# Prompt attention of a hybrid decoder layer: value products of two units in one run, and the merge's small products moved to other PSUM banks

## The chip, the cores and the metric

The kernel runs on one core of a Trainium2 chip. A core has five engines that run side by side and are tied together by semaphores only: TensorE (matrix products; PE in the profile, with PEld for its weight loads), VectorE (DVE), ScalarE (ACT), GpSimd (POOL) and SyncE (SP, which here only issues DMAs). [...] The metric is the device time of one execution in microseconds, lower is better.

## The reference, cut to what matters

The kernel computes one layer of a decoder for a prompt of 2048 tokens and for 8 sequences of 8 new tokens: two mixers in parallel (dilated window attention and a gated linear attention), an output projection, and a feed-forward block with a small convolution. The change touches only the prompt's part of the window attention:

```python
PATTERNS = ((128, 1), (512, 4), (2048, 16))     # window, dilation
def dilated_prompt(q, k, v, window, dil):       # 8 heads of 64
    n = window // dil                           # 128 in each pattern
    qb, kb, vb = to_blocks(q), to_blocks(k), to_blocks(v)
    kk, vv = with_prev(kb), with_prev(vb)       # the block before and the block itself
    s = jnp.einsum('brhcie,brhcje->brhcij', qb, kk) * (E ** -0.5)
    s = jnp.where(mask, s, NEG)
    lse = jax.nn.logsumexp(s, axis=-1)
    p = jnp.exp(s - lse[..., None])
    o = jnp.einsum('brhcij,brhcje->brhcie', p, vv)
    ...
def combine_patterns(results):                  # weights: the softmax denominators
    w = jax.nn.softmax(lses, axis=0)
    return jnp.sum(w[..., None] * outs, axis=0)
```

So each of the three patterns has 16 blocks of 128 queries for each head; a block meets the keys of the block before it and its own (the first block of a strided sequence, and every block of the last pattern, only its own). The outputs of the patterns are merged for each head and position with weights from the softmax denominators.

## The kernel before

The program runs in three stages: the projections and the linear attention, the prompt attention (`attention()`, with `at_merge()` and the class `AtUnit`), and the tail (output projection and feed-forward). The framework's scheduler gives each engine the order of its instructions from the data's dependences, program order as priority, and the buffers that are free: each tile has a tag with so many buffers, and a tile takes one when its first instruction is placed. Over that the kernel lays orders of its own: `line()` in `AtUnit` chains all TensorE instructions of the attention units in program order, and `line()` of the layer does so for GpSimd's gathers and merge work. TensorE's products of the merge are in neither chain; the scheduler puts them between.

The work of `attention()`: four head pairs `pr`, each with three patterns `pat`, each with four groups `g` of four blocks. A group is cut into two units of two blocks in patterns 0 and 1, and is one unit of four blocks in pattern 2. So a head pair has 8 + 8 + 4 = 20 units, and all have 80. A unit has three steps:

- `qk_()`, scores: for each of the two heads a PSUM tile `pas` (tag "as"), filled by products of f32r queries with the high and the low part of the keys (L1860; 8 products of up to 256 columns in patterns 0 and 1, 16 of 128 columns in pattern 2). VectorE adds the mask and takes the row's minimum (L1865: `ass`, `aml`; the queries carry a negative sign), ScalarE takes the exponential with the row's sum (L1869). In patterns 1 and 2 the queries come from a tile `aqg` that GpSimd gathers (`at_gather`, L1130), two for each group, two groups ahead.
- `t()`, transposes: for each head up to four 128x128 transposes of `ass` into a PSUM tile `pat` (L1886, tag "apt", two banks); the tile is copied to SBUF (`apt`) by ScalarE (L63) or VectorE (L65), three to two.
- `pv()`, value products: 64 rows of output for each head, head 0 to partitions 0 to 63 and head 1 to 64 to 127, with 128x64 weights (L1903), 12 or 16 products a unit. The PSUM tile `pao` (tag "ao", two banks) belongs to a group: both units of a group fill it in patterns 0 and 1. After the group's last unit VectorE copies it to `aop` (L65), one SBUF tile for each pattern, in five buffers.

A list `fifo` staggers the steps: when unit n has done its scores, unit n-2 does its transposes and unit n-3 its value products. In TensorE's order the steps come as scores(n), transposes(n-2), values(n-3), scores(n+1), and so on.

When the last unit of a head pair has done its value products, `at_merge()` begins for that pair, a generator that goes on by one step with each group of the next pair. It spreads the row minima and sums of patterns 0 and 2 over the positions with eight small products each (L1139 from `ML[0]`, L1142 from `ML[2]`) into one PSUM tile `pam`, which VectorE multiplies with masks (L1148, L1151) and reduces; a chain of small operations of VectorE and one exponential gives the weights, which TensorE transposes (L1194, into `pab`), VectorE copies and GpSimd's queue writes to memory (`awd`, L1199). They are read back spread over partitions (`awb`, L1187), and GpSimd multiplies the outputs with them and adds (L1229, L1214, L1239), in one order with the gathers of the next pair. For the last pair there is no memory trip: weights are copied out by ScalarE and GpSimd (L1222, L1224), transposed by TensorE into `pab` (L1226), and VectorE multiplies from PSUM (L1227).

The eight PSUM banks before: three for "as", two for "apt", two for "ao", one for "am" (`pam` and the first `pab`; in the last merge `pab` goes round "am", "ao", "ao").

Of the kernel before, what the change touches and what calls it, by code (L numbers as in the profile page):

```python
# [10 lines left out]
F32 = mybir.dt.float32  # L11
# [25 lines left out]
class Layer:  # L37
# [370 lines left out]
    def sweep_a(self, c):  # L408
# [39 lines left out]
        for nn in range(2):  # L448
            wv = [self.wget(), self.wget()]
            for t0, m in self.vblocks(c):  # L450
                ps = self.psum.tile([128, 512], F32, name=self.n("pv"), tag="g1", bufs=3)
                self.vgemm(ps, xs, t0, m, wv)
                vs = self.st.tile([128, 256], F32, name=self.n("vs"), tag="vs", bufs=self.AB["vsb"])
                self.evac(vs[:m], ps[:m, :256], "v")
# [499 lines left out]
        yield  # L954


    AB = dict(mw=1, qg=5, vsb=5, mq='p', klh=1, q=2, v=6, s=6, pt=4, op=5, ps=3, ppt=2, po=2, am=1, skew=(2, 3), man=(), ea=3, ed=5, mp=12, aa=(1, 4, 7, 9, 10), ms='pppp', mv=2, em=1)

    def px(self, name, dt=F32):
        return self.pxpool.tile([128, 2 * H], dt, name=self.n(name), tag="px", bufs=4)  # L960
# [22 lines left out]
    def attention(self):  # L983
        with ExitStack() as ctx:
            self.aq[1] = self.pool(ctx, "at1")
            p = self.ap = self.pool(ctx, "at")
            self.app = self.pool(ctx, "atp", bass.MemoryType.PSUM)
            self.ev = 0
            pend = None
            fifo = []  # L990
            sk = self.AB["skew"]

            def drain(n):
                nonlocal pend
                if len(fifo) > sk[0]:
                    fifo[-1 - sk[0]].t()
                while len(fifo) > n:
                    un = fifo.pop(0)
                    un.t()
                    un.pv()  # L1000
                    if un.last:
                        for _ in pend or ():
                            pass
                        pend = self.at_merge(un.pr, un.ML, un.OP)

            if self.AB['man']:
                eng = mybir.EngineType
                ctx.enter_context(self.tc.manual_schedule(engines={getattr(eng, e) for e in self.AB['man']}))
            self.vq = []
            self.at_loadv(0)  # L1010
            self.at_loadv(1)
            for _ in self.at_load(0, ((1, 2),), to=self.qk0):
                pass
            rest = self.at_load(0, ((2, 4),), to=self.qk0)
            self.qgn = []
            for _ in range(self.AB["qg"]):
                p.tile([128, 4, 128], F32R, name=self.n("aqg"), tag="aqg", bufs=self.AB["qg"])
            for pat in range(3):
                for _ in range(2):
                    p.tile([128, 16, 4], F32, name=self.n("aml"), tag=f"aml{pat}", bufs=2)  # L1020
            for _ in range(2):
                p.tile([128, 3, 4, 128], F32, name=self.n("awb"), tag="awb", bufs=2)
            for _ in range(2):
                p.tile([128, 512], F32, name=self.n("amo"), tag="amo", bufs=2)
            pre = iter(())
            for pr in range(4):
                if pr == 3:
                    self.rctx.close()
                    pre = self.wo_pre()
                qk = self.qk0  # L1030
                nxt = self.at_load(pr + 1) if pr < 3 else iter(())
                ML, OP = [], []
                for pat in range(3):
                    base = 16 * (3 * pr + pat)
                    ml = p.tile([128, 16, 4], F32, name=self.n("aml"), tag=f"aml{pat}", bufs=2)
                    op = p.tile([128, 4, 512], F32, name=self.n("aop"), tag="aop", bufs=self.AB["op"])
                    ML.append(ml)
                    OP.append(op)
                    for g in range(4):
                        if base // 4 + g + 2 < 48:  # L1040
                            self.at_loadv(base // 4 + g + 2)
                        for _ in rest:
                            pass
                        po = [None]
                        nu = 1 if pat == 2 else 2
                        for u in range(nu):
                            fifo.append(AtUnit(self, pr, pat, g, u, nu, qk, base, ML, OP, po))
                            fifo[-1].qk_()
                            drain(sk[1])
                            if pat:  # L1050
                                next(pre, None)
                        if pend is not None:
                            next(pend, None)
                        if 5 <= 4 * pat + g < 11:
                            self.qk0 = next(nxt, self.qk0)
            for _ in pre:
                pass
            drain(0)
            for _ in pend:
                pass  # L1060
# [73 lines left out]
    def at_merge(self, pr, ML, OP):  # L1134
        nc, p, pp, AB = self.nc, self.ap, self.app, self.AB
        sel, sm = self.asel, self.asm
        pm = pp.tile([128, 512], F32, name=self.n("pam"), tag="am", bufs=AB["am"])
        for r in range(4):
            nc.tensor.matmul(pm[:, 64 * r:64 * r + 64], sel[r], ML[0].rearrange("p b x -> p (b x)"),  # L1139
                             start=True, stop=True)  # L1140
# [20 lines left out]
        em, line = (nc.gpsimd, lambda x: x) if pr == 3 else (nc.vector, self.line)  # L1161
# [28 lines left out]
            return W  # L1190

        if not last:
            pt = pp.tile([128, 512], F32, name=self.n("pab"), tag="am", bufs=AB["am"])
            nc.tensor.transpose(pt[:96, :128], awf, self.ident)  # L1194
            wt = p.tile([128, 512], F32, name=self.n("awt"), tag="amo", bufs=2)[:96, :128]
            self.evac(wt, pt[:96, :128], "v")
            wd = self.a["awd"][pr]
            yield
            line(nc.gpsimd.dma_start(wd, wt))  # L1199
            yield  # L1200
            nxt = weights(0)
            for _ in range(AB["mw"]):
                yield
        tags = ("am", "ao", "ao")
        j = 0
        for cb in range(4):
            sl = slice(128 * cb, 128 * cb + 128)
            if last:
                W = weights(cb)
            else:  # L1210
                W, nxt = nxt, weights(cb + 1) if cb < 3 else None
            for i in range(3):
                if i == 2 and not last:
                    line(nc.gpsimd.tensor_tensor(OP[1][:, :, sl], OP[1][:, :, sl], OP[0][:, :, sl], op=ALU.add))  # L1214
                    yield
                if last:
                    tg = tags[j % 3]
                    pb = pp.tile([128, 4, 128], F32, name=self.n("pab"), tag=tg, bufs=AB[dict(am="am", ao="po")[tg]])
                    ab = W[:, i].rearrange("p r (h e) -> p r h e", h=2)
                    src = cap(aw, 24 * cb + 4 * i, [[1, 4], [12, 2], [0, 64]])  # L1220
                    if j in AB['aa']:
                        nc.scalar.copy(ab, src)  # L1222
                    else:
                        nc.gpsimd.tensor_scalar(ab, src, 1.0, 0.0, op0=ALU.mult, op1=ALU.add)  # L1224
                    for r in range(4):
                        nc.tensor.transpose(pb[:, r, :], W[:, i, r, :], self.ident)  # L1226
                    nc.vector.tensor_tensor(OP[i][:, :, sl], OP[i][:, :, sl], pb, op=ALU.mult)  # L1227
                else:
                    line(nc.gpsimd.tensor_tensor(OP[i][:, :, sl], OP[i][:, :, sl], W[:, i], op=ALU.mult))  # L1229
                j += 1  # L1230
            if last:
                mo = self.aq[1].tile([128, 512], F32, name=self.n("amo"), tag="ass", bufs=AB["s"])
            else:
                mo = p.tile([128, 512], F32, name=self.n("amo"), tag="amo", bufs=2)
            e, le = (nc.vector, lambda x: x) if last else (nc.gpsimd, line)
            if last:
                e.tensor_tensor(OP[1][:, :, sl], OP[0][:, :, sl], OP[1][:, :, sl], op=ALU.add)
            e, le = (nc.vector, lambda x: x) if last and cb >= AB["mv"] else (nc.gpsimd, line)
            le(e.tensor_tensor(mo.rearrange("p (m r) -> p r m", r=4),  # L1239
                               OP[1][:, :, sl], OP[2][:, :, sl], op=ALU.add))  # L1240
            line(nc.gpsimd.dma_start(self.a["mixa"][:, pr, 512 * cb:512 * cb + 512], mo))
            if last and cb < 2:
                if cb == 0:
                    self.xnext[3] = self.hl()
                o, m = ((0, 512), (512, 2 * H - 512))[cb]
                self.split(*(t[:, o:o + m] for t in self.xnext[3]), mo[:, :m], "v")
            if cb < 3:
                yield
# [807 lines left out]
```

## Time and profile before

| | |
|---|---|
| median of three runs | 2746.82 us (2745.77 to 2751.03) |
| the profiled execution | 2747.31 us; span 2745.3 us, granted clock 0.989 |
| busy over the span | PE 2655.9 us (97%), DVE 1791.5 (65%), ACT 1270.2 (46%), POOL 587.2 (21%) |
| prompt attention | about 770 to 1063 us of the span |

A row of the order of time gives start, length, engine, line, operation, `out<-in`, and in brackets the idle time before it and what ended that. Lengths of TensorE's products overlap, since they are pipelined; what a product costs is read from start to start. In the view of windows each engine has its busy time in a stretch and the number of instructions, then come the clock granted to TensorE (1.00 is full), the share of the DMA engines and GB/s. In the view of waits the columns are total us, times, and the longest.

### The profile page before, as it was taken

To read this page: it belongs to the slowest core of one execution; us is meant where nothing else is said; L and a number is where in the kernel's file an instruction comes from. 1 tells how busy PE (TensorE), PEld (TensorE's weight loads), DVE (VectorE), ACT (ScalarE), POOL (GpSimd) and SP (SyncE) were. 2 spreads that over 40 slices of the span, in tenths; PEclk is the share of its full clock that TensorE was granted. 3 is DMA by queue.
4 is the path that set the end of the run, shared out by engine and by line. 5 is a ranking of instruction groups with operands and counts; after the bars stand their busy time and mean duration, and the time that the engine had idled before them with its cause. 6 is when DMAs were issued, how large, how long until landed. Compare 5 with 4: busy or idle time off the path is not lost. (4 is left out here: it accounts for less than half of the span.)

```text
span 2745.3 us, 58213 instructions
## 1 busy us (share of the span) xinstructions
PE 2655.9 (97%) x22203; PEld 2520.9 (92%) x22203; DVE 1791.5 (65%) x4338; ACT 1270.2 (46%) x2961; POOL 587.2 (21%) x643
## 2 busy tenths in 40 slices
PE   8999999999999998998999998999999999999997
PEld 6899899888788887998999998999999999999997
DVE  7545544444357776468899889865676665766666
ACT  6535433333368784445555455433344332443332
POOL 4435243433345674012000020000110000200001
PEclk9999999999999999999999999999999999999998
DMA  8755436799776663376677588986698766976654
GB/s 316 254 182 190 165 116 218 264 334 370 267 260 193 191 168 108 127 249 258 249 274 288 196 323 299 341 303 207 239 341 289 279 227 211 327 249 216 215 192 148
DMA packets 287015, 661.67 MB, mean 241 GB/s; under 512 B 32960, under 2 KB 82752, under 8 KB 284688
## 3 DMA queue, kind: packets, MB, share of 16 engines
q1 hardware_dynamic: 256528, 579.53, 61.1%
q0 software_dynamic: 13216, 46.56, 5.1%
q10 hardware_dynamic: 16992, 31.86, 3.1%
q8 instruction: 175, 2.87, 0.4%
q14 instruction: 104, 0.85, 0.1%
HBM read 511.45 MB, written 146.37 MB: 240 GB/s over the span
## 5 line engine op out<-in xcount | busy, mean ns | idle before, releaser
L70 ACT ACTIVATE ws<-wr 128x512 fp32r<-128x512 f32 (+1 forms) x482 | 292.8, 616 | 426.2 <-PE pfe L1628 138.6
L92 PE MATMUL pfd<-hh,ws 128*128 128x264 f32 x2816 | 474.6, 285 | 6.8 <-ACT ws L70 5.6
L92 PEld LDWEIGHTS pfd<-hh,ws 128*128 128x128 f32 x2816 | 400.0, 189 | 9.2 <-ACT ws L70 7.4
L73 DVE TENSOR_TENSOR ws<-wr,ws 128x512 fp32r<-128x512 f32 (+1 forms) x482 | 319.4, 668 | 119.5 <-ACT ws L70 115.7
L92 PE MATMUL pfd<-hl,ws 128*128 128x264 f32 x1408 | 301.5, 285 | 1.8 <-DVE hl L73 1.8
L1628 PE MATMUL pfe<-xh,ws 128*128 128x264 f32 x1496 | 290.3, 286 | 12.1 <-DVE u L1615 7.6
L1628 PE MATMUL pfa<-xh,ws 128*128 128x264 f32 x1496 | 289.8, 285 | 4.5 <-ACT ws L70 1.9
L1628 PE MATMUL pfd<-xh,ws 128*128 128x264 f32 x1408 | 289.3, 285 | 2.1 <-ACT ws L70 1.0
L1628 PEld LDWEIGHTS pfe<-xh,ws 128*128 128x128 f32 x1496 | 236.5, 189 | 13.8 <-DVE u L1615 8.4
L1628 PEld LDWEIGHTS pfa<-xh,ws 128*128 128x128 f32 x1496 | 234.9, 188 | 6.0 <-ACT p L1617 2.4
L399 PE MATMUL pv<-wh,xh 128*128 128x256 f32 (+1 forms) x816 | 236.1, 289 | 1.8 <-DVE th L696 1.8
L1628 PEld LDWEIGHTS pfd<-xh,ws 128*128 128x128 f32 x1408 | 231.3, 189 | 3.1 <-ACT ws L70 1.2
L399 PE MATMUL pv<-wh,xl 128*128 128x256 f32 (+1 forms) x816 | 232.2, 285 | 0.0
L399 PE MATMUL pv<-wl,xh 128*128 128x256 f32 (+1 forms) x816 | 232.2, 285 | 0.0
L92 PEld LDWEIGHTS pfd<-hl,ws 128*128 128x128 f32 x1408 | 225.1, 189 | 2.1 <-DVE hl L73 2.0
L1577 POOL DMA_DIRECT2D xl<-d_xst x52 | 28.1, 541 | 830.8 <-PE pfe L1628 495.4
L1869 ACT ACTIVATE ass<-ass,aml 128x256 f32<-128x256 f32 (+1 forms) x384 | 173.5, 454 | 63.7 <-DVE aml L1865 37.9
L1628 PE MATMUL pfd<-xl,ws 128*128 128x264 f32 x704 | 200.6, 285 | 0.7 <-DMA xl<-d_xst 0.7
L92 PE MATMUL pq<-xh,wh 128*128 128x512 f32 (+2 forms) x480 | 170.9, 364 | 10.7 <-ACT xh L234 7.9
L1628 PE MATMUL pfe<-xl,ws 128*128 128x264 f32 x616 | 175.7, 285 | 0.0
L1628 PE MATMUL pfa<-xl,ws 128*128 128x264 f32 x616 | 174.8, 284 | 0.0
L92 PE MATMUL pq<-xl,wh 128*128 128x512 f32 (+2 forms) x480 | 174.0, 364 | 0.0
(335 smaller groups left out, 6531.6 us busy)
## 6 DMA issues: line engine op xcount, KB each, us to landing
ws<-d_wst SPq DMA_DIRECT2D x248, 512.0 KB, 5.2
wr<-in_wu SPq DMA_DIRECT2D x114, 512.0 KB, 5.0
d_wst<-ws SPq DMA_DIRECT2D x88, 512.0 KB, 4.1
wr<-in_wd SPq DMA_DIRECT2D x160, 256.0 KB, 3.8
wr<-in_wt SPq DMA_DIRECT2D x60, 512.0 KB, 7.0
wh<-d_wbs SPq DMA_DIRECT2D x35, 512.0 KB, 5.6
wl<-d_wbs SPq DMA_DIRECT2D x35, 512.0 KB, 5.8
skp<-in_ckt SPq DMA_DIRECT2D x16, 1024.0 KB, 8.1
```

What stands on the lines that cost most here:

```text
L70: h = nc.scalar.activation(hi, src, AF.Copy)
L73: return h, (nc.gpsimd if lo_eng == "p" else nc.vector).tensor_tensor(lo, src, hi.bitcast(F32), op=ALU.subtract)
L92: mm = nc.tensor.matmul(o, ww[:, k, :], xx[:, s0:s0 + n], start=(k == order[0] and i == 0), stop=(k == order[-1] and i == 2))
L399: mm = nc.tensor.matmul(ps[:m, :256], x[:, t0:t0 + m], w[:, k % 4, :], start=(k == 0 and i == 0), stop=(k == KT - 1 and i == 2))
L1577: self.nc.gpsimd.dma_start(t.bitcast(F32), xo[i, z])
L1628: self.lastmm = nc.tensor.matmul(bank[:, :H], w[:, ww, k, :], xx, start=new and k == 0 and j == 0, stop=k == 3 and j == 2, skip_group_chec ...
L1869: ex = nc.scalar.activation(ssb[:, sc:sc + nk], ssb[:, sc:sc + nk], AF.Exp, bias=self.ml[:, idx, h:h + 1], scale=-1.0, accum_out=self.ml[: ...
```

## The change

Units get a running number `i`. The value products are held back while the newest unit's number is odd; with an even one, the two oldest units do their value products one after the other, and the transposes of unit n-2 come behind them instead of ahead. TensorE's order is then, for even n, scores(n), values(n-4), values(n-3), transposes(n-2), and for odd n, scores(n), transposes(n-2). The tag "as" has four banks for three. The tag "am" is gone: `pam` and the first `pab` take banks of "ao"; in the last merge `pab` goes round "as", "ao", "as".

```diff
-    AB = dict(..., op=5, ps=3, ppt=2, po=2, am=1, skew=(2, 3), ...)
+    AB = dict(..., op=5, ps=4, ppt=2, po=2, skew=(2, 3), ...)
...
+            ui = 0
 
             def drain(n):
                 nonlocal pend
-                if len(fifo) > sk[0]:
-                    fifo[-1 - sk[0]].t()
-                while len(fifo) > n:
+                new = fifo[-1 - sk[0]] if len(fifo) > sk[0] else None
+                while len(fifo) > n and not (n and fifo[-1].i % 2):
                     un = fifo.pop(0)
                     un.t()
                     un.pv()
...
+                if new:
+                    new.t()
...
                             fifo.append(AtUnit(self, pr, pat, g, u, nu, qk, base, ML, OP, po))
+                            fifo[-1].i = ui
+                            ui += 1
                             fifo[-1].qk_()
                             drain(sk[1])
...
     def at_merge(self, pr, ML, OP):
-        pm = pp.tile([128, 512], F32, name=self.n("pam"), tag="am", bufs=AB["am"])
+        pm = pp.tile([128, 512], F32, name=self.n("pam"), tag="ao", bufs=AB["po"])
...
-            pt = pp.tile([128, 512], F32, name=self.n("pab"), tag="am", bufs=AB["am"])
+            pt = pp.tile([128, 512], F32, name=self.n("pab"), tag="ao", bufs=AB["po"])
...
-        tags = ("am", "ao", "ao")
+        tags = ("as", "ao", "as")
...
-                    pb = pp.tile([128, 4, 128], F32, name=self.n("pab"), tag=tg, bufs=AB[dict(am="am", ao="po")[tg]])
+                    pb = pp.tile([128, 4, 128], F32, name=self.n("pab"), tag=tg, bufs=AB[dict(ao="po").get(tg, "ps")])
```

More of the change, by code (lines that the diff above doesn't have):

```diff
@@ L954, in gla_sample @@
         yield
-    AB = dict(mw=1, qg=5, vsb=5, mq='p', klh=1, q=2, v=6, s=6, pt=4, op=5, ps=3, ppt=2, po=2, am=1, skew=(2, 3), man=(), ea=3, ed=5, mp=12, aa=(1, 4, 7, 9, 10), ms='pppp', mv=2, em=1)
+    AB = dict(mw=1, qg=5, vsb=5, mq='p', klh=1, q=2, v=6, s=6, pt=4, op=5, ps=4, ppt=2, po=2, skew=(2, 3), man=(), ea=3, ed=5, mp=12, aa=(1, 4, 7, 9, 10), ms='pppp', mv=2, em=1)
     def px(self, name, dt=F32):
```

## The prediction

> **What bounds the kernel now.** I read the page first, then the stretches of prompt attention in the view of windows, then who waited for whom between 770 and 1050 us, and last the order of time on TensorE and GpSimd.
>
> ```profile
> span 2745.3 us, 58213 instructions
> ```
>
> The profiled execution took 2747.31 us, 0.49 above the median of 2746.82; its span is 2745.3. The change touches only prompt attention, 770 to 1063 us. Windows (columns: PE, PEld, DVE, ACT, POOL busy, granted clock):
>
> ```profile
> 783.30:796.50 13.20, 13.20 (x138) 11.84 (x137) 9.51 (x39) 10.76 (x39) 0.18 (x1) 1.00 0.85 292
> 815.40:831.20 15.80, 15.80 (x167) 14.28 (x166) 11.04 (x72) 15.29 (x70) 6.42 (x6) 1.00 0.55 176
> 831.20:855.40 24.20, 24.19 (x245) 21.33 (x243) 22.92 (x95) 19.92 (x74) 1.79 (x3) 1.00 0.75 230
> 880.30:900.80 20.50, 18.05 (x157) 16.44 (x155) 10.81 (x70) 16.17 (x74) 19.64 (x20) 0.83 0.59 159
> 900.80:925.10 24.30, 24.17 (x247) 21.31 (x245) 23.19 (x97) 18.68 (x68) 8.63 (x10) 1.00 0.80 271
> 1041.10:1063.30 22.20, 14.60 (x120) 11.97 (x119) 17.39 (x30) 7.04 (x14) 16.32 (x27) 0.92 0.24 84
> ```
>
> TensorE is full in most of them, but it is the only full engine in the first alone. In pattern 2 of the first head pair ScalarE is busy 15.29 of 15.80 us; in pattern 0 of a later pair, where the small work of the merge runs beside it, VectorE is busy 22.92 of 24.20 and 23.19 of 24.30; in pattern 2 of the second pair TensorE waits and its clock falls to 0.83. What it waits for:
>
> ```profile
> 893.98 0.48 PE L1860 MATMUL pas<-akh,aqg 128*128 128x128 f32 x1 [2.45 <-POOL aqg L1130]
> 853.61 0.53 POOL L1199 DMA_DIRECT2D d_awd<-awt  x1 [27.70 <-PE pao L1903]
> 892.88 2.04 POOL L1130 CAST aqg<-aqs 128x512 fp32r<-128x512 f32 x2
> 923.22 0.54 POOL L1199 DMA_DIRECT2D d_awd<-awt  x1 [15.21 <-DVE awt L65]
> 964.52 2.02 POOL L1130 CAST aqg<-aqs 128x512 fp32r<-128x512 f32 x2
> ```
>
> GpSimd carries the merge's products and the query gathers in one order. From the write of the weights (853.61) to the pair's last gather (892.88 + 2.04 = 894.92) is 41.3 us; the next round is 923.22 to 966.54, 43.3 us. TensorE arrives early at the last gather and waits. So from the second pair on the time is a loop: GpSimd's 41 to 43 us, then what lies between the last gather and the next write (894.92 to 923.22, 28.3 us), most of it VectorE's.
>
> **What the change saves.** Units have running numbers n (20 per head pair, 80 in all). Before, TensorE runs scores(n), transposes(n-2), value products(n-3). After, for even n: scores(n), values(n-4), values(n-3), transposes(n-2); for odd n: scores(n), transposes(n-2). Nothing is removed; there are 40 runs of value products for 80. What a run costs to enter and leave, from the waits and the order of time:
>
> ```profile
> PEld pao L1903 <- issue: 14.5, 73, 2.0
> PEld pas L1860 <- issue: 9.4, 55, 0.2
> PEld pas L1860 <- DVE aml L1865: 0.5, 3, 0.2
> 842.19 1.04 PE L1886 MATMUL pat<-c_ident,ass 128*128 128x128 f32 x8
> 843.15 0.88 PE L1903 MATMUL pao<-apt,av 128*64 128x128 f32 x12
> 843.96 0.38 PE L1860 MATMUL pas<-akh,aqs 128*128 128x256 f32 x1
> 844.18 0.28 PE L1860 MATMUL pas<-akl,aqs 128*128 128x256 f32 x1
> 845.00 1.26 PE L1886 MATMUL pat<-c_ident,ass 128*128 128x128 f32 x8
> 851.32 0.60 PE L1886 MATMUL pat<-c_ident,ass 128*128 128x128 f32 x4
> 851.75 0.27 PE L1194 MATMUL pab<-c_ident,aaw 128*96 128x128 f32 x1
> 851.86 0.60 PE L1886 MATMUL pat<-c_ident,ass 128*128 128x128 f32 x4
> 852.39 1.09 PE L1903 MATMUL pao<-apt,av 128*64 128x128 f32 x16
> 853.41 0.39 PE L1860 MATMUL pas<-akh,aqs 128*128 128x256 f32 x1
> 773.34 0.82 PE L1886 MATMUL pat<-c_ident,ass 128*128 128x128 f32 x6
> 773.92 0.37 PE L1860 MATMUL pas<-akh,aqs 128*128 128x256 f32 x1
> ```
>
> Start to start: four transposes before another 128-column product take 0.43 us (851.32 to 851.75), four before a value product 0.53 (851.86 to 852.39): entering costs 0.10. Sixteen value products take 1.02 (852.39 to 853.41), twelve 0.81 (843.15 to 843.96), so one is 0.053 to 0.055 and a run carries some 0.15 besides. The first score product after them takes 0.22 (843.96 to 844.18) where the other seven take 0.82, 0.117 each (844.18 to 845.00): leaving costs 0.10. Together 0.35 us a run; the two waits of the weight load on "issue", 14.5 / 73 and 9.4 / 55, about 0.2 and 0.17 us, are its trace. Transposes to scores, of which the new order has two in each pair of units, show no such cost: six transposes took 0.58 (773.34 to 773.92), less than 6 x 0.1075. The new neighbours (scores to values, values to transposes) aren't in the trace. Bounds: 0.20 (the two edges alone) and 0.35; I take 0.35, since the 0.15 belongs to a run, whatever its length. [...]
>
> Gross: 40 x 0.35 = 14.0 us. What of it reaches the end:
> - First pair, patterns 0 and 1 (TensorE alone full): six pairs of units, n = 6 to 16, 6 x 0.35 = **-2.1**.
> - Pattern 2: at most 15.80 - 15.29 = 0.5 us in four units, with ScalarE's queue in order; taken as 0.
> - Between a write of the weights and the last gather: 0. GpSimd covers it; the 2.45 us wait grows by what TensorE saves.
> - Between the last gather and the second half of the merge's sums: one run of values fewer in each of three rounds, 3 x 0.35 = **-1.05**.
> - Beside the merge's small work VectorE leaves 24.20 - 22.92 = 1.3 and 1.1 us a round: 0 to 3 x 1.2 = 3.6; taken as 0, because the chain's operations stand in VectorE's queue between the units'.
>
> **What the change adds.** The transposes' two banks: transposes(n-2) of an odd n now come one scores run (8 x 0.117 = 0.94 us) after the previous ones, where a run of values and one of scores lay between (2.0 us).
>
> ```profile
> 790.42 1.03 PE L1886 MATMUL pat<-c_ident,ass 128*128 128x128 f32 x8
> 791.42 0.56 ACT L63 COPY apt<-pat 128x512 f32<-128x512 f32 x1
> 792.39 0.57 ACT L63 COPY apt<-pat 128x512 f32<-128x512 f32 x1
> ```
>
> Here the second bank's copy ends at 792.96. In the new order the next transposes would need that bank at 790.42 + 8 x 0.1075 + 0.94 + 0.43 = 792.65: a wait of 0.31, and the copies queue behind exponentials. Bounds 0 and 0.3 for each pair of units; 0.2 in nine pairs that count, **+1.8**. The fourth score bank has to cover scores that now follow each other across one run of transposes; scores wait 0.5 us in all for VectorE now (3 times, in the waits above), with one scores run free of every other work between two; with four banks for it: 0.
>
> The merge's sums now take a bank from the two of the value products:
>
> ```profile
> L1139 PE MATMUL pam<-aml,atab x32: 218/275/275, 796.5 to 1002.6; 128*128 128x64 f32 x32
> L1142 PE MATMUL pam<-aml,atab x32: 219/275/323, 835.3 to 1041.9; 128*128 128x64 f32 x32
> 899.31 1.53 PE L1903 MATMUL pao<-apt,av 128*64 128x128 f32 x16
> 901.03 1.28 POOL L1214 TENSOR_TENSOR aop<-aop,aop 128x512 f32<-128x512 f32 x1
> 902.65 2.39 DVE L65 COPY aop<-pao 128x512 f32<-128x512 f32 x2
> L65 DVE COPY aop<-pao 128x512 f32<-128x512 f32 x47 | 38.6, 824 | 11.5 <-PE pao L1903 11.3
> ```
>
> The first half of these sums (L1139) is placed when pattern 0's maxima are there, 39 us ahead of the second (L1142), in a bank that nothing else used. If that stays so, one bank is left to the values through patterns 1 and 2. In pattern 1 both units of a run share a bank; in pattern 2 each has its own, so in the run (n = 16 and 17 of each pair) the second waits for the copy of the first. Cheapest 0 (the sums placed late, or the wait inside ScalarE's backlog); dearest as at 899.31: those values ended before 900.84, their copy began at 902.65, after GpSimd's last read of an output buffer (901.03 + 1.28 = 902.31), and a copy takes 0.82 us on the mean: 902.65 + 0.82 - 900.84 = 2.6 us. I take 0.5 four times, nearer the cheap end, as TensorE has slack in pattern 2: **+2.0**. The transposed weights (L1194) need a bank for one product and a 0.28 us copy: 0.
>
> Ends. The scores of the fifth unit wait for keys:
>
> ```profile
> 780.85 0.38 PE L1860 MATMUL pas<-akl,aqs 128*128 128x256 f32 x1 [0.87 <-DMA akl<-d_kl]
> 1062.19 1.32 PE L1226 MATMUL pab<-c_ident,awb 128*128 128x128 f32 x8 [1.58 <-DVE aop L1227]
> ```
>
> The values that stood ahead of them (12 x 0.055 = 0.66) no longer cover that: **+0.5**. In the last merge the products rotate through six banks for three, and the wait of 1.58 us for VectorE can go; but VectorE is busy 17.39 of 22.20 us there and feeds what follows. Bounds 0 and -1.6; **-0.5**. Queues of DMA and GpSimd keep their order.
>
> Sum: -2.1 - 1.05 + 1.8 + 2.0 + 0.5 - 0.5 = **+0.65** on 2747.31, 2747.96; less 0.49 for the median, 2747.5 us.
>
> **Rivals.** Two executions of this kernel differ by up to 5.3 us, so 0.2% (5.5 us) is the line for "no change".
> - *Faster: the saving isn't swallowed.* VectorE's chain also gives up its 1.2 us a round and the last merge its 1.6, and neither copies nor banks make TensorE wait: 3.15 + 3.6 + 1.6 = 8.4 us, 2738.5. For it: 0.35 us is in every run. Against it: ScalarE, VectorE and GpSimd at 95% and more in turn.
> - *Slower: the held bank.* The second value product of pattern 2 waits 2.6 us in three rounds and 1.0 in the first pair (the copy and its start), ahead of the second half of the sums, so that the loop grows: 8.8 in place of 2.0, +7.45 in all, 2754.3. It decides from (5.5 + 1.35) / 4 = 1.7 us in each of the four. For it: 39 us between the two halves. Against it: the scheduler may find no free bank and place the sums late.
> - *The change doesn't do what it says:* the cost hangs on the first products of any new kind of run. Then nothing is saved and the costs stay, +3.8: 2750.6, still within 0.2%.
>
> **How the numbers follow.** No change, with the third rival in it: 0.57. Faster 0.26 (a further 5 us, where 40 runs save nearly all of 14, have 0.05 of that). Slower 0.17. The range leaves out about a tenth at each end: 2739 to 2754; the likeliest case alone is 2743 to 2751.
>
> **What would show it.** Right: values in runs of 28 or 32; "issue" waits of the weight load before them about half of 73; the wait at the last gather longer than 2.45 us; 41 to 43 us from write to last gather unchanged. Wrong: L1139 right beside L1142 in time (then the held bank is no cost); waits of transposes for copies well over 0.2 us a pair; the stretch from last gather to write shorter than 28 us by more than 1 us. I'd be wrong altogether if the scheduler set VectorE's merge chain in another place.

## The result, and the profile after

The changed kernel took 2765.0 us (median of 4 runs, 2762.88 to 2767.45), the kernel before 2746.3 beside it (2741.34 to 2751.03): a ratio of 1.0065, 95% interval 1.005 to 1.008. It is 18.7 us slower, where 2747.5 was forecast with a range that ended at 2754. The profiled execution took 2767.45 us.

```profile
span 2765.4 us, 58199 instructions
```

Of the 20.1 us by which the spans of the two profiled executions differ, 19.0 lie in the attention stage. Scores(n) is the one mark that both orders share, so the table gives the time from the first scores of one unit to those of another (worked out from the order of time on TensorE; the last column ends at the first product behind the attention). Units 0 to 19 are the first head pair; in a later one eight units are pattern 0 (the previous pair's merge is worked out beside them), eight are pattern 1, four are pattern 2.

| us | first pair | pattern 0, pairs 2, 3, 4 | pattern 1, pairs 2, 3, 4 | pattern 2, pairs 2, 3 | last four units and last merge | all |
|---|---|---|---|---|---|---|
| before | 61.2 | 25.2, 25.3, 25.4 | 23.9, 23.8, 24.3 | 20.4, 22.5 | 41.2 | 293.2 |
| after | 60.3 | 32.9, 34.9, 33.2 | 21.7, 21.7, 26.4 | 18.0, 20.2 | 42.8 | 312.2 |

Pattern 0 of the three later pairs takes 25.1 us more, the rest 6 us less. Some 2.5 us of both only changed place: the first eight of the sums' products, 0.84 us a round, stood in pattern 1 before (860.55 us) and stand in pattern 0 of the next pair now (840.99). The same in the view of windows (PE, PEld, DVE, ACT, POOL busy, then the granted clock), pattern 0 of the second and third pair; in the kernel before, TensorE was busy 25.24 of 25.25 us in the first of the two:

```profile
829.60:862.50 32.90, 26.96 (x270) 25.05 (x269) 24.86 (x101) 21.18 (x81) 4.88 (x6) 0.90 0.67 198
902.21:937.13 34.92, 28.09 (x270) 25.71 (x269) 24.63 (x101) 20.70 (x78) 15.39 (x16) 0.90 0.78 251
```

TensorE is no longer full there, and its clock has fallen (0.90 in both rows, 1.00 in the kernel before). What it waits for, in the view of waits (engine, tile, line, what ended the wait: us in all, times, longest); line numbers behind the change are 4 higher than before:

```profile
PE pab L1198 <- DVE aaw L1184: 15.9, 3, 5.3
PEld pat L1890 <- issue: 7.5, 40, 0.3
PEld pao L1907 <- issue: 3.3, 7, 2.0
```

The transposed weights, costed at nothing, stand for 15.9 us. Of the short waits of the weight load ahead of value products, 73 before, 7 are left; 40 ahead of transposes are new. The order of time on TensorE around the first of the three waits for the weights:

```profile
840.99 1.00 PE L1143 MATMUL pam<-aml,atab 128*128 128x64 f32 x8
841.83 1.06 PE L1146 MATMUL pam<-aml,atab 128*128 128x64 f32 x8
842.72 1.04 PE L1890 MATMUL pat<-c_ident,ass 128*128 128x128 f32 x8
844.42 0.28 PE L1864 MATMUL pas<-akl,aqs 128*128 128x256 f32 x1
850.04 0.42 PE L1198 MATMUL pab<-c_ident,aaw 128*96 128x128 f32 x1 [5.34 <-DVE aaw L1184]
850.39 3.26 PE L1907 MATMUL pao<-apt,av 128*64 128x128 f32 x28
853.58 1.66 PE L1890 MATMUL pat<-c_ident,ass 128*128 128x128 f32 x8
857.93 1.97 PE L1907 MATMUL pao<-apt,av 128*64 128x128 f32 x32
```

and VectorE's chain from the sums to the weights in that time:

```profile
842.98 0.42 DVE L1152 TENSOR_TENSOR atm<-pam,atab 128x256 f32<-128x256 f32 x1 [0.31 <-issue]
846.90 0.18 DVE L1168 TENSOR_TENSOR amm<-amm,aw 128x32 f32<-128x32 f32 x1
848.26 0.21 DVE L1178 TENSOR_TENSOR adn<-aaw,aw 128x32 f32<-128x32 f32 x1 [0.73 <-ACT aaw L1175]
849.46 0.44 DVE L1184 TENSOR_TENSOR aaw<-aaw,amm 128x32 f32<-128x32 f32 x3
```

Sums and transposed weights now take their banks from the value products' pool of two, and here TensorE's order keeps the order in which the banks were asked for: the sums (all 16 products together), a run of transposes and one of scores, the transposed weights, and only then the next value products. VectorE needs 6.9 us for the weights, from 842.98 to 849.90 (849.46 + 0.44). TensorE stands for 5.34 us, and the value products and transposes behind it, which need nothing of the weights, stand with it. No other product ran in the 5.34 us, and no weight load either: the one of the transposed weights, at 850.01, has 5.52 us of idle time before it. Behind the wait the clock is down, 0.52 from 850 to 855 us: 28 value products take 3.26 us at 850.39, and at full clock 32 take 1.97 at 857.93.

```profile
850.00:855.00 5.00, 4.96 (x38) 4.43 (x38) 1.25 (x3) 0.00 (x0) 3.14 (x4) 0.52 0.59 214
855.00:860.00 5.00, 5.00 (x61) 4.69 (x60) 3.41 (x18) 4.38 (x14) 1.75 (x3) 1.00 0.79 172
```

### The profile page after: what moved, and what is told of

The parts are those of the page before. It is cut to its first block, busy times and chain, and to the rows that moved or that the text cites. A ratio compares the mean times of both kernels' runs of the same rounds, so it can differ in the third digit from the quotient of the medians.

```text
span 2765.4 us, 58199 instructions
## 1 busy us (share of the span) xinstructions
PE 2653.6 (96%) x22203; PEld 2530.7 (92%) x22203; DVE 1795.4 (65%) x4338; ACT 1269.8 (46%) x2961; POOL 585.5 (21%) x643
## 5 line engine op out<-in xcount | busy, mean ns | idle before, releaser
L70 ACT ACTIVATE ws<-wr 128x512 fp32r<-128x512 f32 (+1 forms) x482 | 293.2, 616 | 433.2 <-PE pfe L1632 137.9
L1660 DVE TENSOR_TENSOR acc<-acc,pfd 128x264 f32<-128x264 f32 x304 | 116.4, 422 | 90.9 <-PE pfd L92 90.5
```

What stands on the lines that cost most here:

```text
L70: h = nc.scalar.activation(hi, src, AF.Copy)
L1660: nc.vector.tensor_tensor(acc[m][:, s0:s0 + n], acc[m][:, s0:s0 + n], pz, op=ALU.add)
```

## Experiments

Each ran beside the kernel before on the same chip; ratios are to those runs (medians of before from 2743.0 to 2746.1), with 95% intervals. Two theories were set against each other. A: the transposed weights' product, through the bank that it shares, is what costs. B: it is the order of the units, or the sums.

**order_only**: the new order alone, with the banks as they were.

```
     AB: ps=3, po=2, am=1                      # as before
     pam, pab: tag="am"; tags = ("am", "ao", "ao")
...
+    new = fifo[-1 - sk[0]] if len(fifo) > sk[0] else None
+    while len(fifo) > n and not (n and fifo[-1].i % 2):
...
+    if new:
+        new.t()
```

> Kernel before with the new order of value products alone: scores keep three banks, the merge's sums and transposed weights keep their own bank. Theory A (the loss of 19 us is TensorE standing 5.3 us, three times, at the transposed weights that a value bank has put ahead of value products, the slow clock behind that, and the last merge's sums coming 23 us later): the loss is gone, no wait of TensorE for the weights; with the saving of the first head pair, 2740 to 2748 us, if three score banks cost little; each scores run that follows a transposes run alone then waits for VectorE's reads. Theory B (transposes and scores too close together for the copies and reads): still slower than before, 2755 us or more.

Measured: 2742.03 us, ratio 0.9995 (0.9982 to 1.0007), no change. The third transposed weights stand between transposes and wait for nothing:

```profile
990.59 0.27 PE L1198 MATMUL pab<-c_ident,aaw 128*96 128x128 f32 x1
990.70 1.04 PE L1890 MATMUL pat<-c_ident,ass 128*128 128x128 f32 x8
```

**banks_only**: the changed banks with the old order.

> Kernel after with the old order of value products: four score banks, sums and transposed weights in the banks of the value products. Theory A: slower than before: the transposed weights again stand ahead of value products of the next pair, one run of values later than in the kernel after, so TensorE waits some 2 to 4 us three times, and the last merge's sums come behind most of the last value products: +6 to +18 us, 2752 to 2764. Theory B: as before, 2744 to 2749.

Measured: 2770.43 us, 1.0096 (1.0081 to 1.0111). The banks alone cost 27 us. The transposed weights wait 4.67, 4.68 and 4.68 us, more than was put down for theory A. So the loss comes with the banks, and the new order takes some of it back.

**wtrans_late**: the changed kernel, the transposed weights one step later in the merge's program.

```
+            yield
             pt = pp.tile(... name=self.n("pab"), tag="ao", bufs=AB["po"])
...
             wd = self.a["awd"][pr]
-            yield
```

> Kernel after, with the transpose of the weights one step of the merge (two units) later in program order; the write of the weights keeps its place. Theory A: TensorE meets the transpose two units later, the wait of 5.3 us falls to 0 to 2 us three times and the clock no longer falls behind it; the last merge is untouched: 2748 to 2757. Theory B: 2763 to 2767, as after.

Measured: 2753.37 us, 1.0029 (1.0014 to 1.0044). The waits are 2.24, 2.25 and 2.24 us, a little more than theory A gave. The clock stays up behind the first and the third (32 value products take 1.97 us) and falls to half for 3.4 us behind the second (3.00 us). By the ratios about half of the loss is gone (1.0065 to 1.0029).

**last_sums_as**: the changed kernel, the last pair's sums in a score bank.

> Kernel after, with the sums of the last merge alone in a bank of the scores, which are done by then. Theory A: the sums are ready some 6 us earlier, the last merge starts that much earlier: 2757 to 2762. Rival (the end of attention hangs on the last value products and VectorE's copies of them, not on the sums): 2764 to 2766.

Measured: 2760.99 us, 1.0063 (1.0039 to 1.0087). The last sums come 8 us earlier in the stage, VectorE begins on them 4 us earlier, and the stage ends no earlier (313.3 us against 312.2): the last merge doesn't hang on them. The median lies in the theory's range, but the kernel before also ran 3.3 us lower beside this one than beside the change; the ratios, 1.0063 and 1.0065, show no gain.

**weights_own**, **sums_own**, **shared_three**: three score banks, and the freed bank for the transposed weights alone, for the sums alone, or for nothing.

```
weights_own:  ps=3, am=1;  pam: tag="ao";  pab: tag="am"
sums_own:     ps=3, am=1;  pam: tag="am";  pab: tag="ao"
shared_three: ps=3;        pam: tag="ao";  pab: tag="ao"
```

> The changed kernel with three score banks again and the freed bank for the transposed weights alone; the sums stay in a value bank. In the order of issue the one product of the transposed weights then stands between two runs of transposes, behind two more units, and not ahead of a run of values. Theory A (the loss of 18.7 us is this product, which stands in TensorE's order 5.3 us before its operand is ready, three times, and the clock that falls behind it): the three waits are under 0.5 us, the clock stays at 1.00 there, and the time falls to 2744 to 2752. Rival B (the sums in a value bank are what costs, since they come late and all together): the waits go but the time stays above 2756. The last merge keeps its bank order, so if its loss is separate (from the last write of the weights to the end of attention 81.1 us in the changed kernel, 68.4 before), 2750 to 2756, with 74 us or more in that stretch.

> The mirror image: three score banks, the freed bank for the merge's sums alone, the transposed weights stay in a value bank. The sums go back to two halves, some 40 us apart. Theory A: the product of the transposed weights still waits three times for VectorE's weights, 3 to 5.5 us each, and the time stays at 2754 to 2766. Rival B: the time is within 4 us of before (2743), whatever that product waits.

> The changed kernel with three score banks; the fourth is left unused, sums and transposed weights stay in the value banks. It prices the fourth score bank by itself. Theory A (the bank hides little, since scores follow each other across one run of transposes): within 5 us of the changed kernel, 2760 to 2770, with waits of scores for VectorE of 1 to 1.5 us once or twice a head pair. Rival: the fourth bank is what lets TensorE run on, and without it the scores wait in each pair of units, 0.3 us in 40 of them: 2774 and more.

| kernel | sums | transposed weights | us | ratio | pattern 0, pairs 2, 3, 4 |
|---|---|---|---|---|---|
| order_only | own | own | 2742.03 | 0.9995 (0.9982 to 1.0007) | 25.2, 27.0, 26.5 |
| weights_own | shared | own | 2749.58 | 1.0011 (1.0001 to 1.0022) | 25.8, 26.6, 26.5 |
| sums_own | own | shared | 2755.24 | 1.0032 (1.0021 to 1.0044) | 27.7, 34.2, 33.3 |
| shared_three | shared | shared | 2763.45 | 1.0061 (1.0043 to 1.0079) | 32.8, 34.9, 33.3 |

By the ratios the transposed weights' shared bank costs 0.50% (1.0061 less 1.0011) where the sums share too and 0.37% where they don't, 10 to 14 us; the sums' shared bank costs 0.16% and 0.29%, 4 to 8 us. A difference of two ratios is uncertain by about 0.2% here, so the weights' cost is clear of noise and the sums' only just. The two together are the loss, and the fourth score bank is worth nothing: with it 1.0065, without it 1.0061. In weights_own the product is at 851.76 us, between transposes and a whole pair of units behind the sums, with the weights ready 1.7 us before. From the last write of the weights to the end of attention weights_own takes 70.1 us (81.1 in the changed kernel, 68.4 before), so most of the loss in that stretch came from the same product and was not separate. In sums_own the product waits again:

```profile
PE pab L1198 <- DVE aaw L1184: 12.7, 3, 5.0
```

**one_value_bank**: four score banks, one value bank, the merge's bank kept.

```
AB: ps=4, po=1, am=1;  pam, pab: tag="am"
```

> The bank for the fourth score bank taken from the values in place of the merge: four score banks, one value bank, sums and transposed weights in one bank of their own, last merge in five banks. It prices a held value bank, the slower rival of the prediction: in pattern 2 the second unit of each run of values waits for the copy of the first. Rival of the prediction (2.6 us in each such run of a later pair): two runs a head pair, 2 x 2.6 x 3 and 2 x 1.0 in the first = 17.6 us more than with two value banks, 2757 to 2765. If the wait is nearer the 0.5 us that was put in the sum, 8 x 0.5 = 4: 2744 to 2750. In patterns 0 and 1 a run starts 5.7 us after the last one and a copy takes 0.82, so no wait is expected there.

Measured: 2761.51 us, 1.005 (1.0033 to 1.0067), where the prediction's slower rival gave it 2757 to 2765:

```profile
PE pao L1907 <- DVE aop L65: 13.9, 5, 3.9
```

A value run that finds its only bank held by a copy waits some 3 to 4 us: 3.06 and 3.91 us in the third pair's first units (values of pattern 2 of the pair before), 6.8 in all at the same place in the fourth. The second pair has one of 2.93 us there, at 844.13, which the view puts down to another operation of VectorE, though the copy of that bank ended at 844.07. The price of that rival (2.6 us) was near. It did not occur in the change, because the sums were not placed early.

**before_light**, **order_light**: where the saved runs go. Both orders, with the old banks and without the additions of one output buffer to another.

```
-    line(nc.gpsimd.tensor_tensor(OP[1][:, :, sl], OP[1][:, :, sl], OP[0][:, :, sl], op=ALU.add))
```

> The kernel before without the sum of two output buffers in the merges of the first three head pairs: the four additions of aop to aop on GpSimd (1.28 us each) are left out, so the first pattern's share is missing from those pairs. It shortens GpSimd's chain from the write of the weights to the last gather (41.4 us in the last pair) by up to 5.1 us in each of three rounds. Theory A (in the kernel before this chain ends about together with TensorE's own work, TensorE waits 2.0 us at the last gather): the chain shortens, the waits at the last gather go, and the time falls by 3 x 2 and a little more, 5 to 10 us: 2734 to 2740. Rival: the gathers are not what holds TensorE, and nothing changes (within 3 us).

> The new order with the tags' old banks (three score banks, sums and transposed weights in one of their own), and the same additions left out. With them the new order gained nothing (2742.0 against 2743.0). Theory A (what the 40 saved runs bring is swallowed by GpSimd's chain of 41 us in each of three rounds): here more of it reaches the end, and the new order is 4 to 10 us faster than the kernel before with the same omission. Rival (what is saved on the edges of the runs goes elsewhere: to the waits of scores for the third bank, to copies of the transposes, to VectorE's chain): the two orders again agree within 3 us.

Measured: 2727.31 us, 0.9933 (0.9916 to 0.9951), and 2729.86 us, 0.9943 (0.9928 to 0.9958). Taking 5.2 us a round (4 x 1.30) off GpSimd's chain saves 18.8 and 16.2 us: it does set the time of the kernel before. That is more than the 5 to 10 expected and than the 15.6 us taken off in three rounds: with the waits at the gathers the stretches of fallen clock behind them go too (in before the clock is at half for 6.83 us from 893.41 and from 965.09; in before_light it stays up in pattern 2 of both pairs, 1.00 from 850 to 892 us and from 914 to 957). But the new order gains nothing here either. TensorE does its work in less time in it (busy 262.5 us of the stage for 267.0), and waits instead:

```profile
766.64:1041.58 274.94, 266.98 (x2685) 0.99 0.67 195
766.40:1045.55 279.15, 262.48 (x2686) 0.97 0.65 192
947.56 0.33 PE L1863 MATMUL pas<-akh,aqg 128*128 128x128 f32 x1 [2.54 <-POOL aqg L1134]
```

(the first row is the stage of before_light in the view of windows, TensorE alone; the other two are of order_light). The lighter chain still holds the new order at one gather.

**before_light2**, **order_light2**: also without the product of pattern 1 with its weights.

```
-                else:
+                elif i != 1:
                     line(nc.gpsimd.tensor_tensor(OP[i][:, :, sl], OP[i][:, :, sl], W[:, i], op=ALU.mult))
```

> The kernel before with two parts of the merge left out in the first three head pairs: the sum of two output buffers, as in the lighter kernel above, and the product of the second pattern with its weights (4 more operations of 1.28 us on GpSimd a pair). Theory A (GpSimd's chain swallowed the saving; in the lighter kernel TensorE is already busy 270.6 us of its attention stage of 274.9, so it is the bound there): nothing more is gained, 2723 to 2729. Rival: GpSimd still held it, and it gains up to 15 us more.

> The new order with the old banks and the same two parts left out. Theory A: the wait of 2.54 us at a gather and the fallen clock behind it go, TensorE's saving of 7 us in busy time and more reaches the end: 2716 to 2723, 4 to 10 us less than the old order with the same omission. Rival (the new order has a cost of its own: copies of the transposes, the third score bank, the last pair): within 3 us of the old order.

Measured: 2728.21 us, 0.9935 (0.9922 to 0.9948), and 2724.16 us, 0.9921 (0.9908 to 0.9933). The old order gains nothing more: TensorE, busy 267.0 us of its stage as in before_light, is its bound. The new order is 4 us ahead, at the low end of the difference expected; its time lies just above the range of 2716 to 2723, and the two intervals overlap, so the gain isn't clear of noise. The stage of the profiled executions shows where it would come from:

| us | first pair | pattern 0 | pattern 1 | pattern 2 | last four and merge | all |
|---|---|---|---|---|---|---|
| before_light2 | 61.7 | 25.2, 25.3, 25.3 | 23.9, 23.8, 24.3 | 15.0, 15.0 | 36.7 | 276.1 |
| order_light2 | 59.6 | 25.2, 25.5, 25.5 | 22.5, 22.5, 26.3 | 14.3, 14.4 | 37.2 | 273.1 |

In pattern 1, where TensorE alone is full, the eight units take 22.5 us for 23.85: 0.34 us for each of four saved runs (0.18 to 0.40; most often a pair of units takes 5.25 us for 5.64). In pattern 0 nothing is saved; VectorE is busy 23.7 of 25.2 us there, so it probably sets that time, which no run tried.

**order_old_last**, **old_last_six**: the new order with old banks, the old order in the last pair; and the same with the last merge in score and value banks.

```
+    if new and fifo[-1].i >= 60:
+        new.t()
-    while len(fifo) > n and not (n and fifo[-1].i % 2):
+    while len(fifo) > n and not (n and fifo[-1].i % 2 and fifo[-1].i < 60):
old_last_six also:
-    tags = ("am", "ao", "ao")
+    tags = ("as", "ao", "as")
```

> The new order with the old banks in the first three head pairs, the old order (transposes, then the value products of one unit) in the last pair. In the profiles the new order reached the first scores of the last pair after 196.6 us, the old one after 202.4, and the last pair to the end of attention then took 95.3 and 90.9. If that loss belongs to the order in the last pair, where other work stands beside it on ScalarE and VectorE: 4 us less than the new order throughout, 2736 to 2740. Rival (the last pair's time is set by GpSimd's chain from the third write of the weights, 41 us in both): no more than 1.5 us off, 2741 to 2744.

> The same as the one before, and the last merge's products rotate through the score banks and the value banks (five here) in place of the merge's own and the value banks (three), as the change has it. The prediction put this step of the change at 0.5 us saved, bounds 0 and 1.6. Expected 0 to 1.6 us less than without it; a loss above 1 us would say that the scores' banks come free later than the merge's own.

Measured: 2742.58 us, 0.9988 (0.9977 to 0.9999), and 2744.79 us, 0.9997 (0.9987 to 1.0007). The last pair is not given back by its own order (from unit 60 on 96.4 us, 95.3 with the new order throughout, 90.9 before), so the rival holds. The last merge's banks show no gain; a loss above 1 us can't be told from none.

**before_vadd**, **order_vadd**: the whole computation, the additions on VectorE.

```
-    line(nc.gpsimd.tensor_tensor(OP[1][:, :, sl], ...
+    nc.vector.tensor_tensor(OP[1][:, :, sl], ...
```

> The kernel before, whole, with the additions of two output buffers in the merges of the first three pairs moved from GpSimd to VectorE. GpSimd's chain becomes 5 us a round shorter, VectorE gets 4 operations a pair, estimated at 0.6 to 1.3 us each. Theory A: most of the 18.8 us that leaving them out brought, 2728 to 2738. Rival: the additions land in VectorE's queue among the maxima that ScalarE waits for, and the chain of the merge is handed from GpSimd to VectorE and back: 2740 to 2750.

> The new order with the old banks and the additions on VectorE, whole. Theory A: as the kernel before with the same move, or up to 5 us faster, 2724 to 2738. Rival as there: 2740 to 2750.

Measured: 2745.49 us, 1.0001 (0.9992 to 1.0011), and 2741.51 us, 0.9986 (0.9976 to 0.9996). The theory fell and the rival held: an addition takes 1396 ns on the mean on VectorE (680 at best) and took 1304 on GpSimd, and GpSimd waits for VectorE, in before_vadd:

```profile
L1214 DVE TENSOR_TENSOR aop<-aop,aop 128x512 f32<-128x512 f32 x12 | 16.8, 1396 | 3.3 <-POOL aop L1229 3.3
POOL amo L1239 <- DVE aop L1214: 11.5, 4, 3.9
```

Of the kernels that leave nothing out order_vadd is the best, 0.04 to 0.24% below before.

## Why the prediction was wrong

The step that failed is the sentence "The transposed weights (L1194) need a bank for one product and a 0.28 us copy: 0". It priced what the bank is needed for, and not what stands behind the product in TensorE's order. The product needs VectorE's weights; the value products behind it need nothing of them, but they ask the same two banks for room and came later. Its size: weights_own takes 22 of the 25.1 us in pattern 0 away (7.1, 8.3 and 6.7). Of these 15.9 are the waits; the rest is about what the slow clock takes behind them, an estimate from 6.83 us at half clock each time (from 847.97, 923.06 and 998.15 us): 16 us in all lie behind the waits, which costs up to 8. Some of the 22 us comes back in pattern 2 and in the last four units, so that the whole kernel gains 10 to 14. That chain was there to be read before: the weights' write came 18.3 to 18.4 us behind the second half of the sums in each round, and a product placed two runs behind them had to wait.

The other steps, in the order of the sum:

- *Runs and their price.* Right. Value products run in 28 or 32, the "issue" waits ahead of them went from 73 to 7, and a run is worth 0.34 us on the mean of pattern 1, where TensorE alone is full (0.35 forecast, and not the 0.20 of the edges alone). The 40 new waits ahead of transposes, 7.5 us in all, are the ones that remain.
- *What of it reaches the end.* First pair: -2.1 forecast for its patterns 0 and 1. They take 46.2 us before, 46.3 in the change (where 0.8 us of the sums no longer stand among them), 46.5 in order_only. From the scores of unit 6 to those of unit 16 order_only does save 1.5 us (29.9 to 28.4), but up to unit 6 it loses 1.8 (16.3 to 18.1). The term that was put at +0.5, the scores that wait for keys, was too small: TensorE waits 2.2 us there in order_only and 1.1 in the change (0.9 before), and in the change the clock stands at half from 776.3 to 786.5 us. In the profile of before it doesn't fall there; in before_light and before_light2, with the old order, it is 0.97 on the mean from 766 to 828 us, so part of this may be chance. The 0.9 us that the first pair gains as a whole is of pattern 2. Later pairs, pattern 0: 0 forecast, 0 measured there. Pattern 2: taken as 0, measured 0.6 to 0.7 a round once GpSimd is lighter. GpSimd as the bound of later pairs in the kernel before: shown by before_light. In the change three signs of it failed: the wait at the last gather is 2.0 us and not longer than 2.45, the stretch from a write of the weights to the last gather is 49 to 52 us and not 41 to 43, and the one from there to the next write 25 for 28.
- *Where it goes in order_only.* In part to VectorE's queue. The weights' write comes 18.4 us behind the second half of the sums in the second and third round before (976.49 to 994.91 us the last time), and 22.5 in order_only (970.17 to 992.63): there VectorE takes copies and maxima first and begins on the sums 4.3 us behind them (2.0 before). "I'd be wrong if the scheduler set VectorE's merge chain in another place" is what happened, by 4 us in two of the three rounds.

```profile
976.49 0.78 PE L1142 MATMUL pam<-aml,atab 128*128 128x64 f32 x6
978.52 0.40 DVE L1148 TENSOR_TENSOR atm<-pam,atab 128x256 f32<-128x256 f32 x1
970.17 1.00 PE L1146 MATMUL pam<-aml,atab 128*128 128x64 f32 x8
971.39 2.09 DVE L65 COPY aop<-pao 128x512 f32<-128x512 f32 x2
974.50 0.42 DVE L1152 TENSOR_TENSOR atm<-pam,atab 128x256 f32<-128x256 f32 x1
```

- *Transposes' two banks, +1.8.* Not found in order_only, where transposes wait 2.0 us in all for copies, as before, and the 0.34 a run in pattern 1 is net of any such wait. In the change they wait 4.7 us. *Fourth score bank, 0.* Right (shared_three).
- *The sums in a value bank, +2.0,* and the rival of the held bank. The place was wrong, the size too small. L1143 stands right beside L1146 (840.99 and 841.83), which the prediction named as the sign that the held bank is no cost; so it is, but all 16 products then come late in one piece, and the weights behind them: 4 to 8 us, only just clear of noise.
- *The last merge, -0.5.* No gain shown. With the sums in one piece its first weights are waited for 6.3 us (2.5 in order_only):

```profile
PE pab L1230 <- ACT awb L1226: 6.3, 1, 6.3
PE pab L1230 <- ACT awb L1226: 2.5, 1, 2.5
```

Left open: pattern 1 of the last pair takes 2 us more in the change and in order_light2 (26.4 and 26.3 for 24.3), but not in order_only (24.2) or order_old_last (24.0). What sets it wasn't isolated, nor why the last pair as a whole is longer in the new order. The clock's share of the loss was read from the rows and not tried by itself.

## What to carry to other kernels

When an operation is moved into a pool of buffers that another stage uses, it takes a place in that stage's order too: ask what its operand waits for and what stands behind it, not only how long it holds the buffer. A small product that depends on another engine's chain belongs in a bank of its own (weights_own 1.0011, shared_three 1.0061), or later in the program (wtrans_late, one step later: 1.0029 for 1.0065, with 2.24 us left of each wait). A saving on the fullest engine was worth here what the next fullest allowed: GpSimd's chain first (order_only 0.9995 with 40 runs fewer), then, by its 23.7 us busy of 25.2, probably VectorE. When the last pair begins, the new order is 5.8 us ahead in order_only and in order_light2; in that pair it gives back 4.5 us of it in the one and 2.8 in the other.

## What was unexpected of the hardware

In these runs the length of a wait doesn't say by itself whether the clock falls. Of three of 2.24 and 2.25 us (wtrans_late) the first and the third left TensorE at full speed, the second was followed by 3.41 us at half. One of 2.02 in the kernel before, ahead of 1035.31 us, and one of 2.54 in order_light were followed by a fall too, and not at once: in before the clock stands at half from 1036.77 us, and in order_light the first scores behind the wait take 0.28 us each, from 948.47 on 0.41. The rows are of wtrans_late (the first two waits and the window behind the second, TensorE alone), of order_light, and the window of before:

```profile
851.13 0.29 PE L1199 MATMUL pab<-c_ident,aaw 128*96 128x128 f32 x1 [2.24 <-DVE aaw L1184]
851.34 1.97 PE L1907 MATMUL pao<-apt,av 128*64 128x128 f32 x32
920.34 0.28 PE L1199 MATMUL pab<-c_ident,aaw 128*96 128x128 f32 x1 [2.25 <-DVE aaw L1184]
920.55 3.00 PE L1907 MATMUL pao<-apt,av 128*64 128x128 f32 x32
921.32:924.73 3.41, 3.41 (x28) 0.50 0.75 230
948.06 0.28 PE L1863 MATMUL pas<-akh,aqg 128*128 128x128 f32 x1
948.47 0.41 PE L1863 MATMUL pas<-akl,aqg 128*128 128x128 f32 x1
950.52 3.26 PE L1906 MATMUL pao<-apt,av 128*64 128x128 f32 x28
...
1037.70:1041.00 3.30, 3.30 (x27) 2.88 (x27) 1.54 (x9) 2.86 (x14) 2.98 (x3) 0.62 0.20 78
```

By the clock records of the traces of before and of the change, the clock in the attention stage is either full or half. At half it stands in before for 6.83 us from 893.41 and from 965.09, and for 3.41 us from 1036.77 and from 1053.84; in the change for 10.24 us from 776.29, and for 6.83 us each from 847.97, 923.06, 974.26, 998.15 and 1069.83. What brings it down, and why waits of one length end differently, was not shown.
